# A hybrid decoder block on one core: gated branch results stored unsplit, spatial mixing queued from the first merge branch's first half

## The chip, the cores and the metric

The kernel runs on one core of one Trainium2 chip, as one program. The metric is the device time of an execution in microseconds. Before the change the median of three runs is 1132.85 us (1130.49 to 1134.23).

## The reference

One layer of a decoder block on x of 1024 tokens by 1024 channels, with a memory of 256 rows, all in float32:

```
h = rms_norm(x, norm_w)
a_u, a_v, a_z, b_q, b_k, b_v, b_z, m_q, m_z, g = split(h @ w_in)
u = gelu(a_u); vv = layer_norm(gelu(a_v))
y_a = chunked_spatial_gating(u, vv, a_spatial_w, a_spatial_b) * silu(a_z)   # 768 wide
y_b = window_attentions_combined(b_q, b_k, b_v) * silu(b_z)                 # 256 wide
y_m = cross_attention(m_q, memory) * silu(m_z)                              # 512 wide
merged = gates[0] * (y_a @ proj_a) + gates[1] * (y_b @ proj_b) + gates[2] * (y_m @ proj_m)
out = x + merged @ w_out
```

The spatial gating mixes, within chunks of 128 tokens, the tokens of vv by a causal 128x128 matrix per group of 192 channels, adds a bias and multiplies by u. The three window attentions (dilations 1, 4, 16) are weighed by the softmax of their log-denominators.

## The kernel before, in words

**Products.** Every large product is done in split form: an operand is kept as a high part (rounded to fp32r) and a low part (the rest), and `mm3` (L159 to L161) issues three matmuls, high by high, low by high and high by low. The parts are made by `split` (L137: a cast on ACT for the high part; L138: a subtract on DVE for the low part). Weights go through `piece`: a load from DRAM into a buffer ws (L142, 4 buffers), then `split` into wh and wl (9 buffers each); `take` keeps a few prepared pieces ahead. The last transposed projection (products named t, 690 to 875.7 us of the trace) combines weight loads by sums on DVE first (L343, L344: s<-ws_t).

**Order of the work.** All functions are nested in one function; a list of closures, `queue`, holds small steps of another stage. `pump()`, called after each split product, runs some of them, and `spread(n)` sets the pace so that what is queued is spread over n calls. Each engine runs its instructions in program order. All loads are issued by SyncE (SP), the stores of the stages here by POOL's queue.

**Cross-attention and window sums, pumped into the last transposed projection.** `att_m(j)` handles 128 tokens of mixer M: `load`, `scale`, `load_z` (L708: um.z, the gate silu(z_M), from scr_zm), `s0` to `s3`. `s3` multiplies the attention's result into um.z (L753), splits it and stores both parts (L758) to two DRAM arrays, scr_ymh and scr_yml. `combine(j)` does the window sums: `load` (L771 to L774: three attention results into cb, the gate into um.zb, which lies in the same buffer mz as um.z), `sums` (L781 to L797) and `turn` (two transposes into PSUM yt, L802, multiplied by um.zb into cb's second part, L804, split, two stores, L809). There is one um.z, one um.zb and one cb.

**Merge.** `gates_m` (gates[2]): for each half i of the tokens (512) and each of 8 output tiles dt, twelve matmuls over four channel groups of ym, then DVE adds one to the gate and multiplies (L1163). The gate rows are loaded by `load_gate` (L1136) and ym by `load_y` (L1118), high and low parts as separate loads of 512 KB. `gates(1, ...)` is the branch of y_b: per dt a gate load tg (L1183, 3 buffers), per half six matmuls over yb, DVE's evacuation into tg (L1204) and POOL's addition into merged (L1205). `gates(0, ...)` is the branch of y_a. The products of all three go into PSUM tiles "pj", four buffers.

**Spatial mixing** makes y_a, `spatial(i)` for six slices of 128 channels: `vhat` scales VV on ACT (L1213, eight instructions), `load` brings u (L1221, us, 3 buffers), `half(h)` does the mixing matmuls (L1239, eight for a slice that lies in one group, sixteen narrow ones for slices 1 and 4, into PSUM mx, two buffers), the bias on DVE (L1240, mt), the product with u on POOL (L1244) and the split into ya (yah, yal). `spatial_steps` queues the loads of VV (`load_v`) and the 24 steps and calls `spread(56)`. Before the change `gates_m` calls it in its second half at dt 0, and the loads that it needs (`load_spatial`, `load_v(0)`) are issued there.

Of the kernel before, what the change touches and what calls it, by code (L numbers as in the profile page):

```python
# [12 lines left out]
F32 = mybir.dt.float32  # L13
# [8 lines left out]
P = 128  # L22
# [19 lines left out]
def hybrid_block(  # L42
# [75 lines left out]
    def page(shape, name, dtype=F32, tag="pg", **kw):  # L118
        return pages[-1].tile(shape, dtype, name=name, tag=tag, **kw)
# [16 lines left out]
    def split(hi, lo, y, eng=None):  # L136
        A.copy(out=hi, in_=y)  # L137
        (eng or V).tensor_tensor(out=lo, in0=y, in1=hi.bitcast(F32), op=ALU.subtract)  # L138
# [339 lines left out]

    oscr = [dram.tile([S, 264], F32, name=f"oscr{g}") for g in range(3)]
    scr_k, scr_vm = (dram.tile([2, P, 512], F32, name=n) for n in ("scr_k", "scr_vm"))  # L480
    scr_ym = [dram.tile([P, 4, S], F32R, name=f"scr_ym{c}") for c in "hl"]
    scr_yb = [dram.tile([P, 2, S], F32R, name=f"scr_yb{c}") for c in "hl"]
    queue = deque()

    pace = [0.0, 0.0]
# [1 line left out]
    def spread(slots):  # L487

        pace[0], pace[1] = len(queue) / slots, 0.0
# [204 lines left out]
    def att_m(j):  # L694
# [52 lines left out]
        def s3():  # L747
            po = ps.tile([P, 512], F32, name=f"po_{nm}", tag="tr")
            for h in range(4):
                hs = slice(h * P, (h + 1) * P)  # L750
                for b in range(2):
                    T.matmul(po[:, hs], lhsT=um.x[:, b, hs], rhs=c.pT[b][:, hs], start=b == 0, stop=b == 1)
            V.scalar_tensor_tensor(out=um.z, in0=um.z, scalar=0.5, in1=po.rearrange("p (h t) -> p h t", t=P),  # L753
                                   op0=ALU.mult, op1=ALU.mult)
            y = [wpool.tile([P, 4, P], F32R, name=f"y{d}_{nm}", tag=f"w{d}", bufs=9) for d in "hl"]
            split(y[0], y[1], um.z)
            for d in range(2):
                G.dma_start(out=scr_ym[d][:, :, j * P:(j + 1) * P], in_=y[d])  # L758

        c.load, c.scale, c.load_z, c.s0, c.s1, c.s2, c.s3 = load, scale, load_z, s0, s1, s2, s3  # L760
        return c
# [1 line left out]
    def combine(j):  # L763
# [35 lines left out]
        def turn():  # L799
            pt = ps.tile([P, 512], F32, name=f"yt{j}", tag="tr")  # L800
            for hp in range(2):
                T.transpose(pt[:, hp * P:(hp + 1) * P], cb[:, 0, hp * P:(hp + 1) * P], ident)  # L802
            y = cb[:, 1, 0:256]
            V.scalar_tensor_tensor(out=y, in0=um.zb, scalar=0.5, in1=pt[:, :256],  # L804
                                   op0=ALU.mult, op1=ALU.mult)
            yb = [wpool.tile([P, WW], F32R, name=f"yb{d}{j}", tag=f"w{d}", bufs=9)[:, :256] for d in "hl"]
            split(yb[0], yb[1], y)
            for d in range(2):
                G.dma_start(out=scr_yb[d][:, :, j * P:(j + 1) * P], in_=yb[d].rearrange("p (c t) -> p c t", t=P))  # L809

        c.load, c.sums, c.turn = load, sums, turn
        return c
# [299 lines left out]
    ym, yb = [], []  # L1112

    def load_y(i, places, scr, n, name):
        places.append([[page([P, 2, 512], f"{name}{i}{hp}{d}", F32R) for hp in range(n)] for d in "hl"])
        for hp in range(n):
            for d in range(2):
                nc.sync.dma_start(out=places[i][d][hp].bitcast(F32),  # L1118
                                  in_=scr[d][:, 2 * hp:2 * hp + 2, 512 * i:512 * i + 512].bitcast(F32))

    ybs = [lambda i, k=k: (yb[i][0][0][:, k, :], yb[i][1][0][:, k, :]) for k in range(2)]
    yms = [lambda i, k=k: (ym[i][0][k // 2][:, k % 2, :], ym[i][1][k // 2][:, k % 2, :]) for k in range(4)]
# [11 lines left out]
    def load_gate(i, dt):  # L1134
        t = slice(512 * i, 512 * i + 512)
        nc.sync.dma_start(out=merged[dt][:, t], in_=scr_g[2][dt][:, t])  # L1136

    load_y(0, ym, scr_ym, 2, "ym")
    for dt in range(KT):
        load_gate(0, dt)  # L1140
    spw = p1([P, 4, P], "spw", "spw", 1)
# [6 lines left out]
    def gates_m():  # L1148

        w = []  # L1150
        for i in range(2):
            t = slice(512 * i, 512 * i + 512)
            for dt in range(KT):
                if i == 0:
                    w += take(1, 4)
                pp = ps.tile([P, 512], F32, name=f"pp2{dt}{i}", tag="pj", bufs=4)
                for k in range(4):
                    c = slice(k * P, (k + 1) * P)
                    yh, yl = yms[k](i)
                    mm3(pp, w[dt][0][:, c], w[dt][1][:, c], yh, yl, k == 0, k == 3)  # L1160
                    pump()
                m = merged[dt][:, t]
                V.scalar_tensor_tensor(out=m, in0=m, scalar=1.0, in1=pp, op0=ALU.add, op1=ALU.mult)  # L1163
                if i == 0:
                    if dt == 1:
                        load_y(1, ym, scr_ym, 2, "ym")
                    if dt >= 2:
                        load_gate(1, dt - 2)
                elif dt == 0:
                    load_gate(1, 6)  # L1170
                    load_gate(1, 7)
                    load_spatial()
                    load_v(0)
                    spatial_steps()
                elif dt in (2, 4):
                    load_y(dt // 2 - 1, yb, scr_yb, 1, "yb")

    def gates(br, wp, nk, ys, order=tuple(range(KT)), done=None):
        ahead = deque()
# [69 lines left out]
    def spatial_steps():  # L1249
        for i in range(1, 6):  # L1250
            queue.append(lambda i=i: load_v(i))
        stream([(lambda i=i: spatial(i)) for i in range(6)], (0, 1, 2, 3))
        spread(56)

    gates_m()
    gates(1, w_pb, 2, ybs)
# [246 lines left out]
```

## Time and profile before

| | |
|---|---|
| median of three runs | 1132.85 us (1130.49 to 1134.23) |
| profiled execution | 1130.12 us, span 1128.4 us, mean granted clock 0.993 |
| PE busy | 1094.5 us (97% of the span), 6680 matmuls |
| PE weight loads (PEld) | 955.2 us (85%) |
| DVE busy | 802.7 us (71%), 1693 instructions |
| ACT busy | 514.6 us (46%), 1127 instructions |
| POOL busy | 237.4 us (21%), 278 instructions |
| DRAM traffic | 109.99 MB read, 51.37 MB written, 143 GB/s over the span |

Shares of busy time are means over stages with different limits. What bounds one stage is read from busy times by stretch of the span and from the waits: an instruction's idle time before it, with the instruction that released it. The clock is given as a share of 2.4 GHz; 0.50 is 1.2 GHz. "x" is a count, and in a group's row the busy total stands before the mean of one in ns.

### The profile page before, as it was taken

How to read it: one execution, taken by the hardware profiler on the slowest of the kernel's cores; microseconds unless marked ns; L12 is line 12 of the kernel's file. 1: busy time of each engine (PE TensorE's matmuls, PEld its weight loads, DVE VectorE, ACT ScalarE, POOL GpSimd, SP SyncE). 2: the span in 40 equal slices, each digit the busy share in tenths (PEclk: the TensorE clock that was granted, in tenths of full speed). 3: DMA queues.
4: the chain of work that ended last, by engine and by line, in shares of the span. 5: the costliest groups of instructions: out<-in, count | busy, mean ns of one | idle time of the engine just before them, and what ended most of it. 6: DMA issues, size and time to landing. Idle time of an engine off the chain costs nothing. (4 is left out here: it accounts for less than half of the span.)

```text
span 1128.4 us, 18378 instructions
## 1 busy us (share of the span) xinstructions
PE 1094.5 (97%) x6680; PEld 955.2 (85%) x6680; DVE 802.7 (71%) x1693; ACT 514.6 (46%) x1127; POOL 237.4 (21%) x278
## 2 busy tenths in 40 slices
PE   8989999999999999999999999999999998898998
PEld 7779999999988887888888888888888786786898
DVE  6979898866787765766556656688877249759873
ACT  6644333223245543655566554767655072223320
POOL 0000421421000002011111111122121017656332
PEclk9989999999999999999999999999999999999999
DMA  6322423454242434444444335476765995522432
GB/s 197 108 91 76 150 75 104 144 188 150 76 135 94 131 107 130 141 132 151 127 136 133 108 105 189 124 184 175 185 146 157 376 297 196 173 94 65 141 110 79
DMA packets 95951, 160.20 MB, mean 142 GB/s; under 512 B 9733, under 2 KB 43124, under 8 KB 95860
## 3 DMA queue, kind: packets, MB, share of 16 engines
q1 hardware_dynamic: 69796, 110.01, 31.5%
q0 software_dynamic: 24624, 46.53, 12.9%
q10 hardware_dynamic: 1440, 2.49, 0.6%
q8 instruction: 52, 0.85, 0.3%
q14 instruction: 39, 0.32, 0.1%
HBM read 109.99 MB, written 51.37 MB: 143 GB/s over the span
## 5 line engine op out<-in xcount | busy, mean ns | idle before, releaser
L159 PE MATMUL t<-th,wh_t 128*128 128x512 f32 x336 | 135.2, 402 | 0.0
L161 PE MATMUL t<-th,wl_t 128*128 128x512 f32 x336 | 132.0, 393 | 0.0
L160 PE MATMUL t<-tl,wh_t 128*128 128x512 f32 x336 | 131.5, 391 | 0.0
L159 PE MATMUL n<-wh_n,th 128*128 128x256 f32 x384 | 108.0, 282 | 0.0
L160 PE MATMUL n<-wl_n,th 128*128 128x256 f32 x384 | 107.7, 281 | 0.1
L161 PE MATMUL n<-wh_n,tl 128*128 128x256 f32 x384 | 107.5, 280 | 0.0
L161 PEld LDWEIGHTS t<-th,wl_t 128*128 128x128 f32 x336 | 63.1, 188 | 14.4
L159 PEld LDWEIGHTS n<-wh_n,th 128*128 128x128 f32 x384 | 73.0, 190 | 1.7 <-issue 0.9
L160 PEld LDWEIGHTS t<-tl,wh_t 128*128 128x128 f32 x336 | 63.2, 188 | 12.7
L159 PEld LDWEIGHTS t<-th,wh_t 128*128 128x128 f32 x336 | 63.3, 188 | 12.3
L160 PEld LDWEIGHTS n<-wl_n,th 128*128 128x128 f32 x384 | 72.3, 188 | 0.7 <-DVE wl_n L138 0.3
L161 PEld LDWEIGHTS n<-wh_n,tl 128*128 128x128 f32 x384 | 72.2, 188 | 0.0
L159 PE MATMUL t<-H2h,wh_t 128*128 128x512 f32 x168 | 67.8, 403 | 0.0
L161 PE MATMUL t<-H2h,wl_t 128*128 128x512 f32 x168 | 66.0, 393 | 0.0
L160 PE MATMUL t<-H2l,wh_t 128*128 128x512 f32 x168 | 65.6, 390 | 0.0
L137 ACT CAST wh_t<-ws_t 128x512 fp32r<-128x512 f32 x86 | 51.8, 620 | 27.5 <-PE n L161 11.5
L138 DVE TENSOR_TENSOR wl_t<-ws_t,wh_t 128x512 fp32r<-128x512 f32 x86 | 58.0, 683 | 8.0 <-ACT wh_t L137 8.0
L948 POOL TENSOR_TENSOR on<-on,nss 128x1024 f32<-128x1024 f32 x12 | 26.1, 2190 | 177.7 <-DVE nss L134 119.8
L1047 POOL DMA_DIRECT2D scr_g<-o x48 | 27.9, 582 | 162.0 <-ACT o L1033 150.3
L1078 DVE TENSOR_TENSOR o<-t,sa 128x512 f32<-128x512 f32 x63 | 43.2, 685 | 25.7 <-PE t L161 24.0
L159 PE MATMUL n<-wh_n,H2h 128*128 128x256 f32 x192 | 54.8, 286 | 0.0
L1033 ACT ACTIVATE o<-o,gb 128x512 f32<-128x512 f32 x48 | 34.7, 723 | 43.3 <-DVE o L1078 43.3
(379 smaller groups left out, 3258.7 us busy)
## 6 DMA issues: line engine op xcount, KB each, us to landing
ws_t<-in_w_t SPq DMA_DIRECT2D x64, 256.0 KB, 3.6
scr_g<-o POOLq DMA_DIRECT2D x48, 256.0 KB, 3.2
tg<-scr_g SPq DMA_DIRECT2D x16, 512.0 KB, 3.3
ws_n<-in_w_n SPq DMA_DIRECT2D x24, 256.0 KB, 3.6
wr_n<-in_w_n SPq DMA_DIRECT2D x24, 256.0 KB, 3.3
scr_qk<-on POOLq DMA_DIRECT2D x12, 512.0 KB, 4.4
bx<-scr_qk SPq DMA_DIRECT2D x24, 256.0 KB, 3.3
wr_t<-in_w_t SPq DMA_DIRECT2D x20, 256.0 KB, 3.3
```

Of the source, the lines that this page charges most:

```text
L137: A.copy(out=hi, in_=y)
L138: (eng or V).tensor_tensor(out=lo, in0=y, in1=hi.bitcast(F32), op=ALU.subtract)
L159: T.matmul(o, lhsT=ah, rhs=bh, start=first, stop=False)
L160: T.matmul(o, lhsT=ah, rhs=bl, start=False, stop=False)
L161: T.matmul(o, lhsT=al, rhs=bh, start=False, stop=last)
L948: G.tensor_tensor(out=v, in0=v, in1=ss[:, 16 * ORD[q]:16 * ORD[q] + 16].unsqueeze(2) .to_broadcast([P, 16, 64]), op=ALU.mult)
L1033: A.activation(out=d, in_=d, func=AF.Tanh, scale=0.5, bias=gb[:, col:col + 1])
L1047: G.dma_start(out=t[:, h], in_=d)
L1078: V.tensor_tensor(out=o[q], in0=psum, in1=s, op=ALU.add)
```

## The change

1. `s3` and `turn` no longer split. Each writes its product in place, into um.z and um.zb, and stores it once, as float32, to one array scr_ym or scr_yb. So the stores read the buffers into which the next tile's gate is loaded.
2. `load_y` loads only that one array, into the page of the low part. A new `split_y` makes the high part by ACT and the low part in place by DVE, one 128x512 piece at a time: four at the head of the merge, four of the second half of ym in `gates_m` at i 0 (dt 4 to 7), four of yb at i 1 (dt 4 to 7).
3. ym's second half, the spatial constants and the first VV are loaded at i 0, dt 0; gate rows of the second half from dt 1 on; `spatial_steps` is called at i 0, dt 2, and spreads over 78 calls, not 56. So 111 instead of 162 branch matmuls stand ahead of the first mixing matmul, five instead of three of its twelve halves fall into `gates_m`, and seven instead of nine into `gates(1)`.

```diff
--- before.py
+++ after.py
@@ -478,8 +478,8 @@
 
     oscr = [dram.tile([S, 264], F32, name=f"oscr{g}") for g in range(3)]
     scr_k, scr_vm = (dram.tile([2, P, 512], F32, name=n) for n in ("scr_k", "scr_vm"))
-    scr_ym = [dram.tile([P, 4, S], F32R, name=f"scr_ym{c}") for c in "hl"]
-    scr_yb = [dram.tile([P, 2, S], F32R, name=f"scr_yb{c}") for c in "hl"]
+    scr_ym = dram.tile([P, 4, S], F32, name="scr_ym")
+    scr_yb = dram.tile([P, 2, S], F32, name="scr_yb")
     queue = deque()
 
     pace = [0.0, 0.0]
@@ -752,10 +752,7 @@
                     T.matmul(po[:, hs], lhsT=um.x[:, b, hs], rhs=c.pT[b][:, hs], start=b == 0, stop=b == 1)
             V.scalar_tensor_tensor(out=um.z, in0=um.z, scalar=0.5, in1=po.rearrange("p (h t) -> p h t", t=P),
                                    op0=ALU.mult, op1=ALU.mult)
-            y = [wpool.tile([P, 4, P], F32R, name=f"y{d}_{nm}", tag=f"w{d}", bufs=9) for d in "hl"]
-            split(y[0], y[1], um.z)
-            for d in range(2):
-                G.dma_start(out=scr_ym[d][:, :, j * P:(j + 1) * P], in_=y[d])
+            G.dma_start(out=scr_ym[:, :, j * P:(j + 1) * P], in_=um.z)
 
         c.load, c.scale, c.load_z, c.s0, c.s1, c.s2, c.s3 = load, scale, load_z, s0, s1, s2, s3
         return c
@@ -800,13 +797,9 @@
             pt = ps.tile([P, 512], F32, name=f"yt{j}", tag="tr")
             for hp in range(2):
                 T.transpose(pt[:, hp * P:(hp + 1) * P], cb[:, 0, hp * P:(hp + 1) * P], ident)
-            y = cb[:, 1, 0:256]
-            V.scalar_tensor_tensor(out=y, in0=um.zb, scalar=0.5, in1=pt[:, :256],
+            V.scalar_tensor_tensor(out=um.zb, in0=um.zb, scalar=0.5, in1=pt[:, :256],
                                    op0=ALU.mult, op1=ALU.mult)
-            yb = [wpool.tile([P, WW], F32R, name=f"yb{d}{j}", tag=f"w{d}", bufs=9)[:, :256] for d in "hl"]
-            split(yb[0], yb[1], y)
-            for d in range(2):
-                G.dma_start(out=scr_yb[d][:, :, j * P:(j + 1) * P], in_=yb[d].rearrange("p (c t) -> p c t", t=P))
+            G.dma_start(out=scr_yb[:, :, j * P:(j + 1) * P], in_=um.zb.rearrange("p (c t) -> p c t", t=P))
 
         c.load, c.sums, c.turn = load, sums, turn
         return c
@@ -1112,11 +1105,14 @@
     ym, yb = [], []
 
     def load_y(i, places, scr, n, name):
+
         places.append([[page([P, 2, 512], f"{name}{i}{hp}{d}", F32R) for hp in range(n)] for d in "hl"])
         for hp in range(n):
-            for d in range(2):
-                nc.sync.dma_start(out=places[i][d][hp].bitcast(F32),
-                                  in_=scr[d][:, 2 * hp:2 * hp + 2, 512 * i:512 * i + 512].bitcast(F32))
+            nc.sync.dma_start(out=places[i][1][hp].bitcast(F32), in_=scr[:, 2 * hp:2 * hp + 2, 512 * i:512 * i + 512])
+
+    def split_y(i, places, k):
+        hi, lo = (places[i][d][k // 2][:, k % 2, :] for d in range(2))
+        split(hi, lo, lo.bitcast(F32))
 
     ybs = [lambda i, k=k: (yb[i][0][0][:, k, :], yb[i][1][0][:, k, :]) for k in range(2)]
     yms = [lambda i, k=k: (ym[i][0][k // 2][:, k % 2, :], ym[i][1][k // 2][:, k % 2, :]) for k in range(4)]
@@ -1136,6 +1132,8 @@
         nc.sync.dma_start(out=merged[dt][:, t], in_=scr_g[2][dt][:, t])
 
     load_y(0, ym, scr_ym, 2, "ym")
+    for i in range(4):
+        split_y(0, ym, i)
     for dt in range(KT):
         load_gate(0, dt)
     spw = p1([P, 4, P], "spw", "spw", 1)
@@ -1162,18 +1160,22 @@
                 m = merged[dt][:, t]
                 V.scalar_tensor_tensor(out=m, in0=m, scalar=1.0, in1=pp, op0=ALU.add, op1=ALU.mult)
                 if i == 0:
-                    if dt == 1:
+                    if dt == 0:
                         load_y(1, ym, scr_ym, 2, "ym")
-                    if dt >= 2:
-                        load_gate(1, dt - 2)
+                        load_spatial()
+                        load_v(0)
+                    if dt >= 1:
+                        load_gate(1, dt - 1)
+                    if dt == 2:
+                        spatial_steps()
+                    if dt >= 4:
+                        split_y(1, ym, dt - 4)
                 elif dt == 0:
-                    load_gate(1, 6)
                     load_gate(1, 7)
-                    load_spatial()
-                    load_v(0)
-                    spatial_steps()
-                elif dt in (2, 4):
-                    load_y(dt // 2 - 1, yb, scr_yb, 1, "yb")
+                elif dt in (1, 2):
+                    load_y(dt - 1, yb, scr_yb, 1, "yb")
+                elif dt >= 4:
+                    split_y(dt // 2 - 2, yb, dt % 2)
 
     def gates(br, wp, nk, ys, order=tuple(range(KT)), done=None):
         ahead = deque()
@@ -1250,7 +1252,7 @@
         for i in range(1, 6):
             queue.append(lambda i=i: load_v(i))
         stream([(lambda i=i: spatial(i)) for i in range(6)], (0, 1, 2, 3))
-        spread(56)
+        spread(78)
 
     gates_m()
     gates(1, w_pb, 2, ybs)
```

The order of instructions moves at three places. The first is SP in `gates_m`, around the first VV load. In the names, merged is a gate row, VV and us are mixing operands, tg a gate of branch 1, ws_p a weight, and numbers count buffers. Before, the second half's eight gate rows end here:

```order
L1136 DMA merged_9477<-scr_g_691 128x512
L1136 DMA merged_9478<-scr_g_692 128x512
L1136 DMA merged_9479<-scr_g_693 128x512
L1145 DMA spw<-scr_sw 128x512
L1146 DMA off<-scr_off 128x768
L1110 DMA VV_9678<-scr_av 128x8x128
L1110 DMA VV_9687<-scr_av 128x8x128
```

and with the change:

```order
L1111 DMA ym10l<-scr_ym 128x2x512
L1111 DMA ym11l<-scr_ym 128x2x512
L1143 DMA spw<-scr_sw 128x512
L1144 DMA off<-scr_off 128x768
L1103 DMA VV_9456<-scr_av 128x8x128
L1132 DMA merged_9390<-scr_g_686 128x512
L1132 DMA merged_9391<-scr_g_687 128x512
L1103 DMA VV_9516<-scr_av 128x8x128
```

The first VV load now stands ahead of the second half's eight gate rows, the later ones stand among them, and of ym four loads instead of eight stand ahead of it.

The second place is DVE at the end of `gates_m` and the start of branch 1 (wl_p 128x256 are that branch's narrow weight subtracts, tg its evacuations, mt and yal the mixing). Before, from the second tile's first half on:

```order
L1204 SCALAR_TENSOR_TENSOR tg_9870<-tg_9870,pp_9926 128x512
L138 TENSOR_TENSOR wl_p_9963<-ws_p_9960,wh_p_9962 128x256
L138 TENSOR_TENSOR wl_p_10007<-ws_p_10004,wh_p_10006 128x256
L1204 SCALAR_TENSOR_TENSOR tg_9870<-tg_9870,pp_9947 128x512
L138 TENSOR_TENSOR yal_9931<-mt_9933,yah_9930 128x512
L1204 SCALAR_TENSOR_TENSOR tg_9918<-tg_9918,pp_9966 128x512
L1240 SCALAR_TENSOR_TENSOR mt_9988<-mx_9987,colt,off 128x512
L1204 SCALAR_TENSOR_TENSOR tg_9918<-tg_9918,pp_9983 128x512
L138 TENSOR_TENSOR wl_p_10047<-ws_p_10044,wh_p_10046 128x256
L138 TENSOR_TENSOR wl_p_10091<-ws_p_10088,wh_p_10090 128x256
```

and with the change, up to the first tile's first half:

```order
L138 TENSOR_TENSOR wl_p_9965<-ws_p_9962,wh_p_9964 128x256
L1161 SCALAR_TENSOR_TENSOR merged_9396<-merged_9396,pp_9788 128x512
L138 TENSOR_TENSOR wl_p_10017<-ws_p_10014,wh_p_10016 128x256
L138 TENSOR_TENSOR yal_9796<-mt_9798,yah_9795 128x512
L138 TENSOR_TENSOR wl_p_10045<-ws_p_10042,wh_p_10044 128x256
L138 TENSOR_TENSOR wl_p_10097<-ws_p_10094,wh_p_10096 128x256
L1161 SCALAR_TENSOR_TENSOR merged_9397<-merged_9397,pp_9816 128x512
L138 TENSOR_TENSOR wl_p_10155<-ws_p_10152,wh_p_10154 128x512
L1206 SCALAR_TENSOR_TENSOR tg_9842<-tg_9842,pp_9858 128x512
```

The eight narrow weight subtracts of branch 1 now all stand before its first evacuation, where five stood behind it. On SP the loads of these weights move ahead with them: the fourth tg load now stands behind ten weight loads and two loads of u that follow the third, before behind two and one.

The third place is DVE in the attention stage, at one tile's window sum (cb) beside a weight sum (s). Before:

```order
L1078 TENSOR_TENSOR o_8224<-t_1_8211,sa_8143 128x512
L793 TENSOR_TENSOR cb<-cb,ew_8175 128x256 x3
L796 TENSOR_TENSOR cb<-cb 128x256
L343 TENSOR_TENSOR s_17_8444<-ws_t_8338,ws_t_8340 128x512
L797 TENSOR_TENSOR cb<-cb 128x256
```

and with the change:

```order
L790 TENSOR_TENSOR cb<-cb,ew_8148 128x256 x3
L793 TENSOR_TENSOR cb<-cb 128x256
L715 SCALAR_TENSOR_TENSOR mq<-qt_m_8140,colt,mq 128x512
L794 TENSOR_TENSOR cb<-cb 128x256
L138 TENSOR_TENSOR wl_t_7_8181<-ws_t_7997,wh_t_7_8180 128x512
L138 TENSOR_TENSOR wl_t_5_8202<-s_16_8118,wh_t_5_8201 128x512
L1071 TENSOR_TENSOR o_8197<-t_1_8184,sa_8116 128x512
L343 TENSOR_TENSOR s_17_8407<-ws_t_8301,ws_t_8303 128x512
```

The weight sum that stood between the two last cb sums now stands four instructions behind them.

## Rows read from the trace of the kernel before

**Rows 1.** Stretches: us, then busy us of PE, PEld, DVE, ACT, POOL; clock, DMA.
```profile
690.00:875.70 185.70, 182.18 (x962) 153.83 (x960) 139.11 (x324) 111.32 (x267) 39.70 (x62) 1.00 0.62 165
875.70:925.60 49.90, 47.69 (x226) 38.55 (x226) 15.27 (x24) 20.66 (x53) 3.12 (x3) 1.00 1.06 361
925.60:945.50 19.90, 18.72 (x109) 15.39 (x107) 15.94 (x21) 5.71 (x13) 13.78 (x11) 1.00 0.50 171
945.50:967.70 22.20, 15.04 (x85) 11.43 (x86) 22.06 (x25) 5.66 (x11) 16.33 (x12) 0.92 0.57 185
967.70:1036.30 68.60, 67.46 (x298) 54.89 (x296) 49.09 (x60) 19.11 (x35) 43.63 (x30) 1.00 0.33 108
```
**Rows 2.** Waits of PE, 690 to 970 us: total us, times, longest.
```profile
PE mx L1239 <- DVE mt L1240: 5.9, 2, 3.8
PE yt L802 <- DVE cb L797: 3.5, 4, 1.2
PE pp L159 <- DVE tg L1204: 2.4, 2, 1.6
PE pp L159 <- DMA ym00h<-scr_ymh: 2.0, 1, 2.0
```
**Rows 3.** Timeline of PE in branch 1: start us, us of one, [idle before].
```profile
956.62 1.16 PE L1239 MATMUL mx<-spw,VV 128*128 128x128 f32 x8 [2.05 <-DVE mt L1240]
...
962.32 2.08 PE L1239 MATMUL mx<-spw,VV 128*128 128x128 f32 x8 [3.84 <-DVE mt L1240]
964.05 0.77 PE L159 MATMUL pp<-yb00h,wh_p 128*128 128x512 f32 x1
```
**Rows 4.** A stretch of one microsecond, columns as in rows 1.
```profile
963.00:964.00 1.00, 1.00 (x7) 1.00 (x7) 1.00 (x2) 0.29 (x1) 1.00 (x2) 0.50 0.99 385
```
**Rows 5.** Timeline of PE, two spatial halves and the products behind them.
```profile
927.71 1.09 PE L1239 MATMUL mx<-spw,VV 128*64 128x128 f32 x16
928.74 0.51 PE L159 MATMUL pp<-yb10h,wh_p 128*128 128x512 f32 x1
...
930.24 1.05 PE L1239 MATMUL mx<-spw,VV 128*128 128x128 f32 x8
931.05 0.48 PE L159 MATMUL pp<-yb00h,wh_p 128*128 128x512 f32 x1
```
**Rows 6.** Timeline of DVE in gates_m, one evacuation.
```profile
895.22 0.69 DVE L1163 SCALAR_TENSOR_TENSOR merged<-merged,pp 128x512 f32<-128x512 f32 x1 [2.06 <-PE pp L161]
```
**Rows 7.** Groups, 690 to 876 us: busy us, mean ns | idle before, releasers.
```profile
L138 DVE TENSOR_TENSOR yl_m<-mz,yh_m 128x512 fp32r<-128x512 f32 x8 | 5.5, 691 | 1.6 <-ACT yh_m L137 1.3
...
L137 ACT CAST yh_m<-mz 128x512 fp32r<-128x512 f32 x8 | 4.9, 618 | 3.8 <-DVE mz L753 3.8
```
**Rows 8.** Timeline of DVE and SP's queue in one attention tile.
```profile
761.07 0.69 DVE L343 TENSOR_TENSOR s<-ws_t,ws_t 128x512 f32<-128x512 f32 x1 [1.93 <-DMA ws_t<-in_w_t]
...
765.21 0.68 DVE L753 SCALAR_TENSOR_TENSOR mz<-mz,po_m 128x512 f32<-128x512 f32 x1
...
769.20 0.37 SPq L708 DMA_DIRECT2D mz<-scr_zm  x1
```
**Rows 9.** DMA issues, 690 to 876 us: KB each, median us to landing.
```profile
scr_ymh<-yh_m POOLq DMA_DIRECT2D x8, 256.0 KB, 4.5
```
**Rows 10.** Timeline of ACT: the first half of the first VV's scaling.
```profile
903.59 1.65 ACT L1213 ACTIVATE VV<-VV,avs 128x128 f32<-128x128 f32 x4
```
**Rows 11.** Groups of branch 1, 925.6 to 967.7 us, DVE.
```profile
L1204 DVE SCALAR_TENSOR_TENSOR tg<-tg,pp 128x512 f32<-128x512 f32 x14 | 9.4, 674 | 0.0
L138 DVE TENSOR_TENSOR wl_p<-ws_p,wh_p 128x256 fp32r<-128x256 f32 x8 | 9.0, 1140 | 0.0
...
L1240 DVE SCALAR_TENSOR_TENSOR mt<-mx,colt,off 128x512 f32<-128x512 f32 x10 | 7.3, 739 | 0.0
L138 DVE TENSOR_TENSOR wl_p<-ws_p,wh_p 128x512 fp32r<-128x512 f32 x4 | 7.1, 1764 | 0.0
...
L138 DVE TENSOR_TENSOR yal<-mt,yah 128x512 fp32r<-128x512 f32 x6 | 6.5, 1084 | 0.5 <-ACT yah L137 0.4
```

## The prediction, as it was put on record

> **What bounds the kernel now.** I read three views in this order: busy time by stretch, then the waits of PE, then the groups and single instructions of the stretch that loses most. The stretches [rows 1] are: the last transposed projection with the attention steps and window sums pumped in (690 to 875.7), merge branch 2 of the reference's gates ("gates_m", to 925.6), branch 1 (to 967.7, cut at 945.5) and branch 0. PE is busy 182.18 of 185.70 us, then 47.69 of 49.90, then only 18.72 of 19.90 and 15.04 of 22.20, then 67.46 of 68.60. So almost everywhere PE itself is the limit, and branch 1 is the exception: 1.2 + 7.2 = 8.3 us lost in 42.1. There DVE is busy 22.06 of 22.20 us: for that half DVE sets the pace. The waits of PE [rows 2] agree: 5.9 us of spatial products behind an earlier DVE evacuation (mt), 2.4 behind the tg evacuations. Outside it there are 3.5 us behind the window sum (cb) and 2.0 for the first ym load.
>
> One event stands out [rows 3]: a spatial product waits 2.05 us, the next one 3.84 us, and that next one, which starts at 962.32, takes 2.08 us where its twin took 1.16; PE's next product starts 1.73 us after it. The granted clock of the microsecond 963 to 964 is 0.50 [rows 4], that is 1.2 GHz, where all the rest runs at 1.00, and the whole half stretch has 0.92 [rows 1]. Against 0.81 between the same two starts at full clock [rows 5] this costs 0.9 us, and the three slow branch products behind it, half their own time, some 0.7 more: 1.6 in all.
>
> **The change, part by part.** Prices of PE: twelve branch products take 2.75 us, the idle plus the busy time of one evacuation that comes once per twelve [rows 6], so 0.229 each. One spatial half costs 0.81 from its start to the next product's, plus 0.1 for that product's slower start, 0.9; with narrow parts (units 1 and 4) 1.03 + 0.1 = 1.1 [rows 5].
>
> 1. *Attention steps and sums without split.* Per token tile DVE loses one 128x512 subtract of 691 ns and ACT one cast of 618 ns [rows 7], and the 128x256 pair, which I cost at half of these. Over eight tiles that frees about 8.3 us of DVE and 7.4 of ACT, where DVE is busy 139.11 and PE 182.18 of 185.70 [rows 1]. So it is hidden, except for the 3.5 us of cb waits [rows 2]. One of these four stands behind a late weight sum s, which itself waited 1.93 us for its weight [rows 8] while the cb sums were queued behind it on DVE; the new order puts the cb sums first at that place. Bounds: 0 (some other late row steps in) and -3.5. I take the middle, **-1.8**.
>
> 2. *Stores that read um.z.* The next reload of um.z now waits on SP for the store's landing. Today the z product ends at 765.21 + 0.68 = 765.89 and the reload of mz issues at 769.20 [rows 8]; a store lands 4.5 us after its issue [rows 9]. With an issue of about 0.8 us (an estimate from the 0.4 to 1 us that issues show) the reload would go at 765.89 + 0.8 + 4.5 = 771.2, 2.0 us later than today. Behind it on SP stand two weight loads. PE has no wait on a weight in this stretch [rows 2] as two prepared pieces lie ahead of it, so the 2.0 us are covered: **0**. If that cover were gone, it is rival C. The z buffer itself is read two steps later, so its own lateness is covered too. POOL issues half as many stores and waits on ACT no more.
>
> 3. *First branch, head.* The first 512 KB load is issued and lands as before (PE waited 2.0 us for it [rows 2]). Now an ACT cast comes between, 618 ns [rows 7], and a signal: **+0.7**. The low part needs one load and the cast and DVE subtract, where before it had a load of its own; it is the second product's operand, 0.2 us later than the first, so at worst a subtract of 0.69 more is seen: bounds +0.6 and +1.3.
>
> 4. *Splits in gates_m.* Twelve splits of 128x512 (four of the first half, four of the second, four of yb): 12 x 0.69 = 8.3 us DVE, 12 x 0.62 = 7.4 us ACT. DVE is busy 15.27 and ACT 20.66 of 49.90 [rows 1]: hidden, 0. Were DVE full, these would be 8.3 us, so what hides them is exactly the idle two thirds of DVE in this stretch. The loads fall from 12 to 6 of 512 KB; the DMA share there is 1.06 at 361 GB/s, but the waits name no load besides the first, so nothing is won directly.
>
> 5. *Spatial mixing earlier.* Five halves instead of three fall into gates_m: one plain and one narrow more, 0.9 + 1.1 = **+2.1** (PE has no slack there). Their data: ahead of the first VV load stand 2 MB of ym and 2 MB of gate rows less, at 361 GB/s some 11 us. Today the scaling of VV begins at 903.59 and takes 2 x 1.65 us [rows 10]; 11 us earlier it is done at about 896. The first half stands after 111 products, at 875.7 + 2.0 + 0.7 + 111 x 0.229 = 903.9. So it does not wait.
>
> 6. *Branch 1.* Seven halves are left, and all eight of the branch's narrow weight subtracts stand ahead of its first tg evacuation on DVE, where five stood among them. PE alone: today's 42.1, less the 2.1 that left, less the clock's 1.6, less all 8.3 of waits: 30.1. DVE: four wide weight subtracts of 1.764, four narrow of 1.140, seven mt of 0.739, seven yal of 1.084 and sixteen tg of 0.674 [rows 11], together 35.2 us. Such rows overlap one another: DVE's groups of this stretch, all summed, come to 41.8 against 15.94 + 22.06 = 38.0 busy, so 35.2 x 0.909 = 32.0. PE may run four branch halves ahead of the last of it, so 32.0 is not a hard floor. I take the middle of 30.1 and 32.0, 31.1: **-11.0**. Bounds: 28.9 from prices alone (96 x 0.229 + 5 x 0.92 + 2 x 1.14), so -13.2; and DVE's 32.0 with the 4.0 us that DVE had idle in the first half stretch today (19.9 - 15.94), 36.0: -6.1.
>
> Branch 0 behind it, PE 67.46 of 68.60 [rows 1], only shifts: 0.
>
> Sum: -1.8 + 0.7 + 2.1 - 11.0 = -10.0, against the profiled execution's 1130.12: 1120.1. The median of the three runs stands 2.7 above that execution, so I give **1122.9** against 1132.85.
>
> **Rivals.**
> - *A. DVE still sets branch 1* (36.0 us instead of 31.1): +4.9, 1127.8. For it: 35.2 us of raw work in some 31 us, DVE full today, and subtracts that take 1140 and 1764 ns [rows 11] where 691 is their price in the attention stretch [rows 7], so beside POOL's work every row is dear. Against: the narrow subtracts move out, and PE can run ahead. 0.20.
> - *B. The later tg loads come late.* The fourth stood behind two weight loads and one load of u on SP; now ten weight loads and two of u stand ahead. If five loads cost PE 1.5 us each: +7.5, 1130.4, no change that can be seen. Against: its buffer is free only after the first tg anyway. 0.08.
> - *C. Slower: store landings on SP starve the transposed projection.* The place is the z reload of part 2. If the 2.0 us reach PE in each of eight tiles, +16: 1138.9. It decides against the change from about 1.3 us per tile (10.0 / 8) on. For: DVE already waits for weights there (1.93 us in one row [rows 8]). Against: PE has not waited for one, and each tile has over 20 us to recover (185.70 / 8). 0.09.
> - *D. The mixing is not really earlier*, because VV comes no sooner than today: scaling done at 903.59 + 3.3 = 906.9, the first half waits 3.0 us, 1125.9. 0.05.
> - *E. The clock falls at a wait that is left.* The row [rows 4] shows 0.50 after waits of 2.05 and 3.84 us with little work between [rows 3]; at the head of gates_m a 2.0 us wait kept 1.00 [rows 1, 2]. There the wait grows to 2.7. If it falls there or once in branch 1, 1.6 us as above: 1124.5. 0.06. The Trainium skill (TensorE: Matmul & The Clock Gate, section "What's actually happening") has the clock go back to its throttled rate when PE has been idle; by that rule the head's longer wait or a remaining DVE wait brings the half rate back, which gives this rival's 1124.5, and the trace so far agrees at 963 us but not at the head.
>
> **How the numbers follow.** Forecast 0.49, A 0.20, B 0.08, C 0.09, D 0.05, E 0.06, something not seen here 0.03. The low end adds the lower bounds (-3.5 + 0.6 + 2.1 - 13.2 = -14.0, 1118.9) and 1.4 for the spread of a median (the three runs span 3.7): 1117.5. The high end is A's 1127.8 with the head's and clock's 1.6 on top, just under 1129.5; B, C and the unseen, 0.20, lie outside. About 0.3%, 3.4 us, can be told from no change: faster means under 1129.5, slower over 1136.2. Faster: nearly all of the forecast (0.47), three quarters of A, D and E: 0.73. Slower: C and most of the unseen, 0.11. The same: the rest, 0.16.
>
> **What would show it.** In the changed profile: branch 1 takes about 31 us with no spatial product waiting over 1 us for mt, the clock 1.00 throughout; gates_m about 52.7 us with the first spatial half near 904; the first product about 0.7 us later after its load; fewer than four cb waits. The sum is wrong if branch 1 exceeds 34 us, or if PE waits on weights between 690 and 870.

## The result and the profile after

The changed kernel takes 1120.49 us (median of 6, 1118.85 to 1122.28); the kernel before, measured beside it, 1132.16 us (median of 6). The ratio is 0.9894, 95% interval 0.9882 to 0.9906: about 1.1% faster. The profiled execution has a span of 1117.5 us against 1128.4 before.

The stretches of the changed kernel, cut at its own stage ends (the end of the transposed projection, the first products of branch 2, branch 1 and branch 0); columns as in [rows 1], whose lines they answer to:

```profile
690.00:869.97 179.97, 179.85 (x958) 153.38 (x956) 132.04 (x307) 105.32 (x250) 27.70 (x46) 1.00 0.50 151
872.30:923.20 50.90, 50.90 (x248) 41.54 (x249) 28.20 (x42) 30.26 (x71) 7.05 (x6) 0.97 0.93 312
923.20:956.90 33.70, 30.31 (x169) 23.64 (x168) 24.06 (x35) 6.71 (x13) 24.23 (x18) 1.00 0.46 148
956.90:1025.40 68.50, 66.54 (x288) 54.03 (x289) 48.07 (x60) 19.36 (x36) 43.40 (x30) 1.00 0.35 117
```

PE is now busy nearly all of the attention stretch, where 3.5 us were lost. Branch 1 takes 33.7 us, not 42.1, and DVE, full in its second half before, is busy 24.06 of 33.70. The second line has a clock of 0.97. The waits of PE from 690 to 1030 us, which answer to [rows 2]:

```profile
PE pp L159 <- DVE tg L1206: 3.1, 4, 1.1
PE mx L1241 <- DVE mt L1242: 2.2, 1, 2.2
PE pp L159 <- ACT ym00h L137: 1.9, 1, 1.9
PE po L159 <- ACT ro L1287: 1.9, 1, 1.9
```

The cb waits are gone, one mx wait is left, those for tg are no shorter, and the head waits for the ACT cast instead of the load. Each stage runs from its first product to the next stage's. The rows of these products, with the first and the last start, before:

```profile
L802 PE MATMUL yt<-ident,cb x16: 270/273/329, 713.8 to 830.2; 128*128 128x128 f32 x16
L159 PE MATMUL pp<-ym00h,wh_p x16: 388/392/470, 877.8 to 898.5; 128*128 128x512 f32 x16
L159 PE MATMUL pp<-yb00h,wh_p x16: 388/432/774, 925.6 to 965.5; 128*128 128x512 f32 x16
L159 PE MATMUL pp<-ya,wh_p x32: 392/392/502, 967.7 to 1031.7; 128*128 128x512 f32 x32
```

and after:

```profile
L799 PE MATMUL yt<-ident,cb x16: 270/271/272, 713.1 to 824.4; 128*128 128x128 f32 x16
L159 PE MATMUL pp<-ym00h,wh_p x16: 388/388/628, 872.3 to 893.9; 128*128 128x512 f32 x16
L159 PE MATMUL pp<-yb00h,wh_p x16: 388/391/505, 923.2 to 953.3; 128*128 128x512 f32 x16
L159 PE MATMUL pp<-ya,wh_p x32: 392/392/502, 956.9 to 1022.0; 128*128 128x512 f32 x32
```

The stages that follow from them (yt is the first transpose of a window sum):

| stage, us | before | after | difference |
|---|---|---|---|
| start to the first yt | 713.8 | 713.1 | -0.7 |
| attention and head wait, to the first ym product | 164.0 | 159.2 | -4.8 |
| gates_m | 47.8 | 50.9 | +3.1 |
| branch 1 | 42.1 | 33.7 | -8.4 |
| branch 0 and output | 160.7 | 160.6 | -0.1 |

The sum is -10.9 in the span. In all kernels below the first yt lies between 713.1 and 717.1, though no instruction that the change or an edit touches lies ahead of it, so the first line is the spread of single executions.

### The profile page after: what moved, and what is told of

Same layout as the page of the kernel before. It is cut to its first block, busy times and chain, and to the rows that moved or that the text cites. A ratio compares the mean times of both kernels' runs of the same rounds, so it can differ in the third digit from the quotient of the medians.

```text
span 1117.5 us, 18284 instructions
## 1 busy us (share of the span) xinstructions
PE 1093.1 (98%) x6680; PEld 955.0 (85%) x6680; DVE 797.3 (71%) x1689; ACT 515.3 (46%) x1123; POOL 224.1 (20%) x262
## 4 chain that ended last, share of the span: by engine, by line
PE 81%; DVE 9%; DMA 3%; POOL 3%; issue 2%; ACT 1%; SPq 0%; DVEq 0%; POOLq 0%; ACTq 0%
PE t L159 11%; PE t L161 11%; PE t L160 11%; PE n L160 7%; PE n L159 7%; PE n L161 7%; PE po L608 3%; PE po L160 2%; PE po L159 2%; PE po L161 2%; PE pp L159 2%; PE pp L160 2%; PE pp L161 2%; POOL merged L1207 2%; PE pt L601 1%
## 5 line engine op out<-in xcount | busy, mean ns | idle before, releaser
L160 PE MATMUL n<-wl_n,H2h 128*128 128x256 f32 x192 | 54.3, 283 | 0.0
```

The costliest lines, as they stand in the source:

```text
L160: T.matmul(o, lhsT=ah, rhs=bl, start=False, stop=False)
```

## The experiments

Twelve kernels ran. The stage times are those of one profiled execution each, read from the same rows; "attention" is the table's second line and holds the wait at the head, 1.4 to 2.8 us (experiment 11 fills it).

**1. Stores alone** (part 3 of the change undone: `spatial_steps`, its loads and those of ym and the gate rows where they were, 56 calls; only the loads of yb stay early).

```diff
-                    if dt == 2:
-                        spatial_steps()
...
                 elif dt == 0:
+                    load_gate(1, 6)
                     load_gate(1, 7)
+                    load_spatial()
+                    load_v(0)
+                    spatial_steps()
...
-        spread(78)
+        spread(56)
```

> The change without its third part: results are stored unsplit, but the mixing is queued in the second half of gates_m as before, over 56 calls. Theory (the mixing's earlier start is what shortens branch 1): branch 1 goes back from 33.7 us to 40 to 42, gates_m loses two mixing halves (-2.1), the attention stretch keeps its 5 us: about 1126.8. Rival (branch 1 is short because its narrow weight subtracts stand ahead of the first tg evacuation, which they do here too, with unsplit stores): branch 1 at 35 to 37, total 1121 to 1123.

Measured: 1126.94 us (ratio to before 0.9955, 0.9935 to 0.9975). Attention 159.4, gates_m 48.7, branch 1 42.3. The theory holds in each stage; the early weight subtracts alone gain nothing in branch 1. The waits of the kernel before are back, with its half clock behind the second:

```profile
PE mx L1241 <- DVE mt L1242: 5.3, 2, 3.7
PE pp L159 <- DVE tg L1206: 3.5, 4, 1.9
```

**2. Mixing alone** (the kernel before with the loop of part 3; stores and loads stay split).

```diff
-                    if dt == 1:
+                    if dt == 0:
                         load_y(1, ym, scr_ym, 2, "ym")
+                        load_spatial()
+                        load_v(0)
...
+                    if dt == 2:
+                        spatial_steps()
...
-        spread(56)
+        spread(78)
```

> The kernel before with the third part alone: split stores and loads stay, the mixing and its loads are queued from the first half's third tile on, over 78 calls. Theory (the earlier mixing shortens branch 1 by itself): attention keeps all four cb waits, the clock stays at 1.00 at the head, gates_m grows by 2.1, branch 1 falls to about 34: 1132.2 + 2.1 - 8.4 = about 1126. Rival (the narrow weight subtracts, which here stay among the tg evacuations, are what counts): branch 1 at 38 to 40, total 1130 to 1132.

Measured: 1127.36 us (0.9958, 0.9947 to 0.9970). Attention 164.2 with all four cb waits, gates_m 51.0, branch 1 34.4. So the shorter branch 1 belongs to the mixing. gates_m grew by 3.2, not 2.1, at full clock; PE waits 0.8 us there for low parts of ym, 0.2 before. Branch 1 holds a fall of the clock to 0.50 here (at 958 to 962 us), as it does before, and is shorter all the same. Alone the two halves of the change gain 4.7 us (experiment 1) and 4.3 us (this one) in the times, both clear of noise. Together they gain 11.7; experiment 1's median is uncertain by some 2 us, and whether the 2.7 us over the sum are real is not shown.

**3. Results to buffers of their own** (the gates' reloads need not wait for the stores).

```diff
-            V.scalar_tensor_tensor(out=um.z, in0=um.z, scalar=0.5, ...
-            G.dma_start(out=scr_ym[:, :, j * P:(j + 1) * P], in_=um.z)
+            y = wpool.tile([P, 4, P], F32, name=f"y_{nm}", tag="wl", bufs=9)
+            V.scalar_tensor_tensor(out=y, in0=um.z, scalar=0.5, ...
+            G.dma_start(out=scr_ym[:, :, j * P:(j + 1) * P], in_=y)
```

(and the same in `turn`)

> The changed kernel, but the two gated products go to buffers of their own, so that the next tile's loads of the gates do not wait for the stores to land. Theory (that wait is covered, since no weight is waited for): same time, 1120.5 within 1 us, DVE waits for s<-ws_t about as long (6.6 us). Rival (it delays weight loads and DVE with them): 1118 to 1119, s<-ws_t waits gone.

Measured: 1120.41 us, the changed kernel's 1120.49. In the changed kernel SP waits long for the stores; the waits of its queue, 700 to 830 us:

```profile
SPq L771 <- DMA scr_yb<-mz: 27.7, 7, 6.9
SPq L768 <- PE yt L799: 24.5, 7, 6.7
SPq L708 <- DMA scr_ym<-mz: 17.7, 7, 9.8
```

and that costs nothing: with those two waits out of the way attention is 159.5.

**4. The splits put back as dead work.**

```diff
             G.dma_start(out=scr_ym[:, :, j * P:(j + 1) * P], in_=um.z)
+            y = [wpool.tile([P, 4, P], F32R, name=f"y{d}_{nm}", tag=f"w{d}", bufs=9) for d in "hl"]
+            split(y[0], y[1], um.z)
```

(and the same in `turn`, from um.zb)

> The changed kernel, with the sixteen splits of the attention stretch put back as work whose results go nowhere; stores and loads stay unsplit. Theory (the casts and subtracts delayed the window sums on DVE): cb waits of PE return, 3 to 5 us, total 1124 to 1125.5. Rival (what went is the order, a weight sum standing ahead of the last cb sum; here no weight sum stands there): cb waits at most 1 us, total 1121.

Measured: 1123.32 us (0.9916, 0.9893 to 0.9938), 2.8 above the changed kernel; attention 160.6. Neither expectation fits whole. No cb wait of PE returned; its only wait in this stretch ahead of the head is the one that opens it:

```profile
PE qt_m L713 <- ACT mx L705: 1.8, 1, 1.8
```

The head wait grew from 1.9 to 2.8 us. So the work of the splits is not what made the window sums late, though it costs time. What else does the change do there? `turn` no longer writes into cb. The waits of SP's queue in the kernel before, 700 to 830 us, show what that did:

```profile
SPq L773 <- DVE cb L797: 30.6, 7, 7.6
SPq L772 <- DVE ybl L138: 21.6, 7, 3.7
```

Line 772 loads cb's second part for the next tile, and stood there until the split's subtract had read that part. This gave the third theory, which the next two kernels test.

**5. The kernel before, with cb free.**

```diff
-            y = cb[:, 1, 0:256]
+            y = um.zb
             V.scalar_tensor_tensor(out=y, in0=um.zb, scalar=0.5, in1=pt[:, :256],
```

> The kernel before with one line changed: turn writes its product into um.zb, where the change has it, not into cb's second part; it is still split and stored in two. Theory (cb's reload had to wait until the split had read cb's second part, which made the next window sums late): no cb waits of PE, the attention stretch falls by 4 to 5 us, total 1127 to 1128. Rival (the removed splits and stores made the gain): cb waits stay at 3 us or more, total 1131 to 1132.

Measured in the profile: attention 160.6, no cb wait. SP's wait for that subtract has moved to the gate's load (line 774), which nobody needs soon:

```profile
SPq L774 <- DVE ybl L138: 35.2, 7, 6.6
```

The loads of the last tile's window sum issue earlier than in the kernel before, 15.4 us ahead of their transpose (at 826.07) instead of 12.0 (at 830.07). SP's queue in the kernel before, then in this one:

```profile
812.64 0.53 SPq L773 DMA_DIRECT2D cb<-oscr  x1
813.26 0.54 SPq L771 DMA_DIRECT2D cb<-oscr  x1
818.09 0.55 SPq L772 DMA_DIRECT2D cb<-oscr  x1
```

```profile
809.45 0.54 SPq L772 DMA_DIRECT2D cb<-oscr  x1
810.09 0.54 SPq L773 DMA_DIRECT2D cb<-oscr  x1
810.72 0.54 SPq L771 DMA_DIRECT2D cb<-oscr  x1
```

But the times do not show the gain: 1130.63 us against 1131.27, ratio 0.9987, interval 0.9972 to 1.0001. Its ten runs span 1126.26 to 1133.63, and the profiled one (1127.16) is among the fastest. The stage is shorter in the profile; that it makes this kernel faster is not shown.

The edit moves something else too. Two of the four waiting sums stood on DVE behind a weight sum (s) that waited for its load, one of them at 761.07 [rows 8]. Now the weight sums stand behind the cb sums, and their waits are no longer PE's. DVE at the same tile in this kernel:

```profile
755.56 0.42 DVE L797 TENSOR_TENSOR cb<-cb 128x256 f32<-128x256 f32 x1
759.77 0.69 DVE L343 TENSOR_TENSOR s<-ws_t,ws_t 128x512 f32<-128x512 f32 x1 [2.59 <-DMA ws_t<-in_w_t]
```

**6. The changed kernel, with cb held.**

```diff
-            V.scalar_tensor_tensor(out=um.zb, in0=um.zb, scalar=0.5, in1=pt[:, :256],
+            y = cb[:, 1, 0:256]
+            V.scalar_tensor_tensor(out=y, in0=um.zb, scalar=0.5, in1=pt[:, :256],
                                    op0=ALU.mult, op1=ALU.mult)
-            G.dma_start(out=scr_yb[...], in_=um.zb.rearrange(...))
+            G.dma_start(out=scr_yb[...], in_=y.rearrange(...))
```

> The changed kernel, with turn's product written into cb's second part again, as before, and stored from there unsplit. No split, half the stores, but the next load into cb waits until the store has landed. Theory (the window sums were late because cb came free late): cb waits of PE return, 3 to 6 us, attention at 163 us or more, total 1124 to 1126. Rival (the work of the splits on DVE and ACT made them late): no cb waits, 1120.5.

Measured: 1126.07 us (0.9941, 0.9925 to 0.9958), 5.6 above the changed kernel: the theory's time, with attention at 162.5, somewhat under its 163. So this one line costs the changed kernel some 5 us. But the cb waits of 3 to 6 us did not come: PE waits 0.8 us for cb and 1.8 us for a late weight.

```profile
PE t L159 <- ACT wh_t L137: 1.8, 1, 1.8
PE yt L799 <- DVE cb L794: 0.8, 1, 0.8
PE qt_m L713 <- ACT mx L705: 0.7, 1, 0.7
```

SP, with the weights' loads queued behind, now waits for the store at cb's load:

```profile
SPq L769 <- DMA scr_yb<-cb: 20.4, 7, 4.3
SPq L770 <- DVE cb L794: 17.6, 4, 8.6
```

and the weight sum stays behind the cb sums although cb is held:

```profile
758.64 0.42 DVE L794 TENSOR_TENSOR cb<-cb 128x256 f32<-128x256 f32 x1
762.25 0.69 DVE L343 TENSOR_TENSOR s<-ws_t,ws_t 128x512 f32<-128x512 f32 x1 [1.98 <-DMA ws_t<-in_w_t]
```

The four cases make a square of stage times: cb held and split 164.0, cb held and not split 162.5, cb free and split 160.6 (both kernels that have it), cb free and not split 159.2 to 159.5. In the stage, freeing cb is worth some 3.3 us and leaving out the splits some 1.3. Two things limit this reading. What holds cb differs, the split's subtract in the kernel before and the store's landing here. And the times agree only where the mixing is early: 1127.36 (held, split), 1126.07 (held, not split), 1123.32 (free, split), 1120.49 (free, not split). In the kernel before, freeing cb gains 0.6 us, and experiment 1, which also leaves out the splits and half the stores, 4.7. How much of the wait was the late load of cb and how much the weight sum ahead of it, no run separates: the two went together in experiment 5, and here the order stayed while cb was held.

**7. The first ym loads cut in two.**

```diff
+            for c in range(2):
+                if (name, i) == ("ym", 0):
+                    nc.sync.dma_start(out=places[i][1][hp][:, c].bitcast(F32), in_=scr[:, 2 * hp + c, ...])
...
```

> The changed kernel, with the two first ym loads of 512 KB cut into four of 256 KB. Theory (PE's wait at the head, and the half clock after it, come from the length of the first load): the wait falls from 2.0 to about 1 us and the clock stays at 1.00: 1118 to 1119. Rival (the loads behind it share the DMA engines, so the first part lands no sooner): wait and total as in the changed kernel, 1120.5.

Measured: 1121.19 us (1121.06 to 1122.65). The head wait fell to 1.4 us and the clock stayed at 1.00, but gates_m is 50.7: the products behind the first now wait briefly for the splits. Two such waits of 0.2 us are named, but from the first ym product to the first mixing product PE takes 26.9 us, 25.6 in experiment 3. No gain.

**8. More mixing in gates_m** (`spread(64)` for `spread(78)`).

> The changed kernel with the mixing spread over 64 calls, not 78: six or seven halves in gates_m. Theory (what is left of branch 1's waits, some 3 us, is DVE held by the low-part subtracts of the mixing): gates_m +1 to +2, branch 1 from 33.7 to 30 or less, total about 1119. Rival (data for the earlier halves come late, or gates_m fills up): a wait before mx in gates_m, total 1121 to 1122.

Measured: 1121.30 us; branch 1 34.7, the clock 1.00 at the head, PE waits 1.3 us for yb's splits in branch 1. No gain, and the theory's fewer halves did not shorten branch 1, though DVE's waits at the low-part subtract fell from 9.9 to 4.3 us. PE is busy 28.89 us in it, 1.4 less than in the changed kernel, but waits 5.8 us, not 3.4: 2.7 for tg, 1.8 for mt and the 1.3 for yb's splits. The rival's wait in gates_m did not come either.

**9. The low part on POOL** (`split(yh[:, t], yl[:, t], mt, G)` in `half`).

> The changed kernel with the mixing's low-part subtract on POOL, not DVE. Theory (DVE stands 9.9 us in branch 1 at that subtract, waiting for POOL and ACT, with tg evacuations queued behind it): DVE is free, branch 1 at about 31 us without mx waits, total 1118. Rival (POOL, busy 24 of 33.7 us there, becomes the bound with about 9 us more): tg buffers come free late, branch 1 at 35 or more, total 1122 to 1124.

Measured: 1123.84 us (0.9924, 0.9909 to 0.9939), branch 1 34.6. The rival's direction, through POOL at 30.87 of 34.60 us; DVE is held no more by the low part but by weights whose casts come late on ACT (10.8 us), and ACT, in order, waits for POOL:

```profile
ACT yah L137 <- POOL mt L1246: 24.0, 6, 6.7
```

**10. The product with u on DVE.**

```diff
-            G.tensor_tensor(out=mt, in0=c.us[:, t], in1=mt, op=ALU.mult)
+            V.tensor_tensor(out=mt, in0=c.us[:, t], in1=mt, op=ALU.mult)
```

> The changed kernel with the mixing's product with u on DVE, not POOL. Theory (DVE's 9.9 us of waits at the low-part subtract in branch 1 come from POOL, where that product queues behind additions into merged): those waits fall under 4 us, branch 1 at 31 to 32 us, total 1118 to 1119. Rival (seven more DVE operations fill DVE): branch 1 at 34 or more, total 1121 to 1123.

Measured: 1117.43 us (0.9862, 0.9844 to 0.9881), branch 1 31.4, the fastest kernel of this study. DVE's 9.9 us of waits at the low part are gone. It is busy all the time now, but not all of that is work: the low-part subtracts take 1772 ns each, 1044 in the changed kernel.

```profile
924.30:955.70 31.40, 29.49 (x170) 23.86 (x168) 31.12 (x39) 6.92 (x13) 18.71 (x13) 1.00 0.49 165
```

```profile
L138 DVE TENSOR_TENSOR yal<-mt,yah 128x512 fp32r<-128x512 f32 x5 | 8.9, 1772 | 0.0
```

**11. A filler at the head.**

```diff
+    fill = ps.tile([P, 512], F32, name="fill", tag="sc")
+    for _ in range(16):
+        T.matmul(fill[:, :P], lhsT=ones, rhs=ones, start=True, stop=True)
     gates_m()
```

> The changed kernel with sixteen small matmuls of ones by ones (128 columns, into a free PSUM buffer) ahead of the first merge product, some 1.7 us of PE work inside its wait of 2.0 us. Theory (the wait lets the clock fall to 0.50 and costs 1.6 us in gates_m): the clock stays at 1.00, gates_m at 49.3, total 1119. Rival (the drop is chance, or the filler delays the first product): 1120.5 to 1122.

Measured: 1122.48 us (1118.55 to 1123.98). The clock stayed at 1.00 and gates_m is 49.2, as the theory says, but the filler itself ran 3.73 us, not 1.7, and the first product follows it:

```profile
873.97 3.73 PE L1259 MATMUL fill<-ones 128*128 128x128 f32 x32
877.45 0.48 PE L159 MATMUL pp<-ym00h,wh_p 128*128 128x512 f32 x1
```

I had taken 0.1 us apiece from the mixing products and counted sixteen. The trace has 32 rows for the sixteen matmuls, as it has eight for the four matmuls of a mixing half, so at the same price the filler takes some 3.2 us. What is gained in the clock is paid at the head, so the theory's gain was not tested as meant.

**12. The kernel before, with the product with u on DVE** (the edit of experiment 10).

> The kernel before with the mixing's product with u on DVE, not POOL, and nothing else. Theory (in branch 1 DVE, busy 22.06 of 22.20 us in the second half, was only apparently full: its subtracts, 1.1 to 1.8 us long, stood behind POOL's operations): with nine POOL operations gone, branch 1 falls from 42.1 to 38 or less, total 1128 or less. Rival (DVE was full with work of its own): nine more operations make branch 1 43 us or more, total 1132 to 1136.

Measured: 1129.31 us (0.9973, 0.9956 to 0.9990): a small gain, less than the theory's. Branch 1 does fall, from 42.1 to 35.4 us, with nine more operations on DVE, so DVE was not full with work of its own. Part of it comes back in branch 0 (165.4 us, 160.7 before), where PE waits for a weight that DVE prepares late, the first row:

```profile
PE pp L161 <- DVE wl_p L138: 3.5, 1, 3.5
PE mx L1239 <- DVE mt L1240: 2.3, 1, 2.3
```

## Why the prediction was right, and where it was not

The forecast was 1122.9 us, the measured time 1120.49, inside the range. The sum of the steps was -10.0 and the span's change is -10.9, but three terms were off and partly cancel, so that the number came so close is partly luck.

- **Part 1 (forecast -1.8, bounds 0 and -3.5):** mis-sized, and beyond its bound. All waits went, and the stage with its head is 4.8 us shorter. The wait rows give PE's idle time alone, 3.5 us; PE's own distances between a tile's first transpose (qt_m) and its yt were 9.46 and 9.61 us in two waiting tiles where 8.26 is normal, 1.2 and 1.35 for waits named as 1.05 and 1.17. Over the eight tiles such losses add up to 5.0 us, the whole gain of the stage. The late weight sum that I had named does stand ahead of two of the four sums and is gone from there, but I took the splits' work for the cause. Experiments 5 and 6 put most of the gain on one line, by which `turn` wrote into cb, which the prediction does not mention; the order that I read moved with that line alone (experiment 5).
- **Part 2 (0):** right. Experiment 3 takes the waits away and the time stays.
- **Part 3 (+0.7):** wrong in its sign at the wait itself: 2.33 us from the last projection product to the first ym product, 2.43 before. The load now lands sooner (PE started 5.1 us after its issue before, the cast starts 4.5 us after it now), which makes room for the cast. But rival E came true in this execution: the clock fell to 0.50 for some 3 us at 874, and gates_m is 50.9 where experiments 3, 9 and 11, without that fall, have 49.3, 49.3 and 49.2. So 1.6 us, E's price. It is not the change's alone: experiment 12, a form of the kernel before, has the fall there too, and experiment 3 has one in branch 1 instead (950 to 954 us).
- **Part 4 (0):** right: DVE is busy 28.20 of 50.90 us and no product waits for a split beyond the first.
- **Part 5 (+2.1):** right. Between experiment 1 and the changed kernel, both with the fall of the clock, gates_m differs by 2.2 us. The first mixing half started at 899.4, 27.1 us after the first ym product; I had 25.5, and the fall's 1.6 us is the difference.
- **Part 6 (-11.0):** mis-sized, -8.4. I took DVE's need from the mean durations of [rows 11]. Its weight subtracts took 416 and 1007 ns, not 1140 and 1764, and it was busy only 24.06 us, not 32.0. Yet branch 1 took 33.7, since DVE stood 9.9 us at the mixing's low-part subtracts, a wait that I had put at nothing. The group of the changed kernel, 923.2 to 956.9 us, beside two of POOL and the weight subtracts:

```profile
L1207 POOL TENSOR_TENSOR merged<-merged,tg 128x512 f32<-128x512 f32 x12 | 16.2, 1356 | 8.8 <-DVE tg L1206 8.8
L1246 POOL TENSOR_TENSOR mt<-us,mt 128x512 f32<-128x512 f32 x6 | 8.9, 1478 | 1.3 <-issue 1.3
...
L138 DVE TENSOR_TENSOR yal<-mt,yah 128x512 fp32r<-128x512 f32 x6 | 6.3, 1044 | 9.9 <-ACT yah L137 9.9
L138 DVE TENSOR_TENSOR wl_p<-ws_p,wh_p 128x512 fp32r<-128x512 f32 x4 | 4.0, 1007 | 0.0
...
L138 DVE TENSOR_TENSOR wl_p<-ws_p,wh_p 128x256 fp32r<-128x256 f32 x5 | 2.0, 416 | 0.0
```

The chain is DVE (mt), POOL (times u, behind the additions into merged in its queue), ACT (cast), DVE (low part), and DVE keeps its order, so the evacuations behind it, mt and tg, are late: PE waits 2.2 us for mt and 1.1 for tg in branch 1. PE's own work was foreseen well, 30.1 us against 30.31 busy; the waits that are left, 3.4 us, are what the sum lacked. Experiment 10 takes POOL out of the chain: 31.4 us, close to the 31.1 that I had put for a branch without that stall; that is in part chance, as DVE then does six more operations. Rival A's time (36.0) was not reached, and its mechanism, DVE full, was not what bound; experiment 12 shows it had not been so before either, since branch 1 got shorter with more work on DVE.

Rivals B, C and D did not come: no wait for a tg load, none of a store's on PE, none at the first mixing product. Of the signs that I had named, two failed: a spatial product still waited 2.2 us for mt, and the clock did not stay at 1.00. Branch 1, at 33.7 us, stayed just under the 34 at which I had called the sum wrong.

What stays open: why the tg evacuations come later in experiment 8, with fewer mixing halves in branch 1 and fewer DVE waits; how much of experiment 5's stage gain a run keeps, since its times scatter; and whether the late load of cb or the order on DVE is what PE felt.

## What to carry to other kernels

A scratch write into part of a buffer that the next tile's load needs holds the load queue until its last reader is done (21.6 us over seven tiles here); look for it when a sum is late. Writing the result over an input that is needed late cost nothing here, although a store has to land first (experiment 3). An engine that looks full may be standing inside its own instructions or behind an in-order wait: compare the mean duration of its rows with the same shape elsewhere before taking "busy" as work. Moving a chain's step to the engine that waits for it can pay even if that engine is the busiest (experiment 10, 3.1 us).

## What the hardware showed that I had not expected

DVE's subtracts in branch 1 seem to wait for POOL's running operation inside their own duration. Timelines of POOL and DVE in the changed kernel:

```profile
951.81 1.30 POOL L1207 TENSOR_TENSOR merged<-merged,tg 128x512 f32<-128x512 f32 x1
...
954.33 1.29 POOL L1207 TENSOR_TENSOR merged<-merged,tg 128x512 f32<-128x512 f32 x1 [1.22 <-DVE tg L1206]
```

```profile
952.53 1.12 DVE L138 TENSOR_TENSOR yal<-mt,yah 128x512 fp32r<-128x512 f32 x1 [1.80 <-ACT yah L137]
953.58 0.67 DVE L1206 SCALAR_TENSOR_TENSOR tg<-tg,pp 128x512 f32<-128x512 f32 x1
```

POOL's addition ends at 953.11, and the subtract, which takes 0.69 us in the attention stage [rows 7], ends at 953.65, 0.54 later, after 1.12. The other four long low-part subtracts of the branch end 0.54 to 0.55 us after a POOL operation as well. The evacuations, of another operation, keep their 0.67. So not every row of DVE is dear beside POOL, as rival A has it. The pattern would explain the means of 1140 and 1764 ns in [rows 11]. It is read from the traces, and no run isolates it.

The fall of the clock at the head of gates_m does not follow from the wait alone: the granted clock fell to 0.50 after waits of 1.9, 2.1 and 2.8 us (the changed kernel, experiments 1 and 4) and stayed at 1.00 after 2.0, 2.2 and 2.3 (the kernel before, experiments 3 and 5). The other kernels add falls after 1.8, 1.9 and 2.3 (experiments 6, 10 and 12) and none after 1.4, 1.5, 1.9 and 2.1 (7, 2, 9 and 8), so waits of 1.9, 2.1 and 2.3 us went either way. The Trainium skill (TensorE: Matmul & The Clock Gate, section "What's actually happening") has the clock follow how busy PE has been lately; experiment 11, which keeps PE busy through the wait, agrees with a clock of 1.00, but one execution beside several that kept it without a filler does not prove it.
